# Feed-forward of a two-layer encoder: one 512-column product for both parts of an activation

## The chip, the cores and the metric

One core of a Trainium2 chip runs the whole program in one launch. The metric is the device time of that launch in microseconds (us). Kernels are compared by the median of several runs. The engines named here are TensorE (PE for its products, PEld for its weight loads), VectorE (DVE), ScalarE (ACT), GpSimd (POOL) and SyncE (SP), which issues nearly all DMAs.

## The reference

Two layers on 256 tokens of width 2048, in float32. Each layer is a token mixer (a gated MLP in layer 0, grouped-query attention in layer 1) followed by a feed-forward; a vector `c` gives each sub-layer a shift, a scale and a gate (`mod`).

```python
for i in range(DEPTH):                                   # DEPTH = 2
    mod = silu(c) @ w_ada[i] + b_ada[i]
    sh1, sc1, gt1, sh2, sc2, gt2 = split(mod, 6)
    h = rmsnorm(x, g_norm[i, 0]) * (1 + sc1) + sh1
    x = x + gt1 * (gmlp(h) if i == 0 else gqa(h))
    h = rmsnorm(x, g_norm[i, 1]) * (1 + sc2) + sh2
    a = h @ w_up[i]                                      # 2048 -> 2 * 5632
    a = cw[0] * a[t - 1] + cw[1] * a[t] + cw[2] * a[t + 1] + cb
    g, val = split(a, 2)
    x = x + gt2 * ((gelu(g) * val) @ w_down[i])          # 5632 -> 2048
return rmsnorm(x, g_final)
```

## The kernel before

**Layout and precision.** Channels lie on the 128 partitions and the 256 tokens (`S`) along the free dimension: `x` is 16 blocks (`NB`) of 128 x 256. Products run on operands of a rounded type (fp32r). To keep the accuracy each operand is split in two: `hi`, the rounded value, and `lo`, the rest. A product of a 128 x 128 weight block with an activation block is then three products that add up in PSUM (`prod_b`): weight hi with activation hi, weight hi with activation lo, weight lo with activation hi. Each has 256 columns and its own weight load. Below, a *block* is one such 128 x 128 weight block with all its products.

**Weights.** `weight` loads a raw tile of up to 2048 columns (5 such buffers), ACT casts it to `hi` in halves of 1024 columns and DVE subtracts to get `lo`; there are 5 half tiles of each. A half tile holds 8 blocks. SP issues the DMAs. The same raw buffers carry the rows of `w_ada`: `ada` reduces one such row block on DVE to 128 values of `mod` (192 of them). The list of all `ada` is worked off by `pump`, called by every `weight`: a credit grows by `state["rate"]` (the constants RO, RK, RU, RD, RW) and each whole credit issues one `ada`.

**Feed-forward** (`ffn`, once per layer). `new_h` and `make_h` give the activation, hi and lo in two tiles, each with rows padded by 8 elements here (`STEP`). The 5632 hidden channels are 44 blocks, each a pair (gate and value). The first 14 pairs begin in `outer`: tiles `pfa` (pairs 0 to 6, half of the sum) and `pfc` (pairs 7 to 13, all of it). Then seven calls of `up_rest` finish pairs 0 to 6, adding to a copy of `pfa` in SBUF (`part`, which is `yacc`), and `up_pair` makes the other 30 pairs (`pf`); both values of a pair share one PSUM bank of 512 columns. `epilogue` does the three-tap convolution, gelu and the product, and `split_f` the hi and lo of the result. The down projection (`pd`) runs in three parts of 16, 16 and 12 pairs (`PARTS`), each over 16 output blocks, once `LEAD` = 2 further pairs have been made; `residual` adds it to `x` (in layer 0 the first part waits in `yacc`). So the order of stages in a layer is pfa, pfc, up 0 (15 weight tiles), down 0 (16 tiles), up 1 (32), down 1 (16), up 2 (20), down 2 (16).

**Order.** The program is written as one sequence. A scheduler then orders the instructions of each engine by its own estimate of times; at run time every engine works strictly in that order. Work on a finished bank is put in `pend` and runs when the next `weight` has issued its casts.

Of the kernel before, what the change touches and what calls it, by code (L numbers as in the profile page):

```python
# [38 lines left out]
RK = ((0.75, 0.75, 0.75, 0.0), (0.6, 0.6, 0.6, 0.0))  # L39
RU = 0.75  # L40
RD = 0.85
RW = 0.5
# [9 lines left out]
def kernel(  # L52
# [20 lines left out]
    def bank(name, tag=None):  # L73
        return cur["ps"].tile([P, 512], F32, tag=tag or cur["tag"], name=name, bufs=cur["bufs"][tag or cur["tag"]])

    def phase(stack, name, nf, bufs={"ps": 8}, tag="ps", rt="ps"):

        cur["ps"] = stack.enter_context(tc.tile_pool(name=name + "_ps", bufs=1,
                                                     space=bass.MemoryType.PSUM, reuse_waits="tile"))
        cur["bufs"], cur["tag"], cur["rt"] = bufs, tag, rt  # L80
        cur["f"] = stack.enter_context(tc.tile_pool(name=name + "_f", bufs=nf, reuse_waits="tile"))
        cur["scr"] = stack.enter_context(tc.tile_pool(name=name, bufs=1, reuse_waits="tile"))
        return cur["scr"]
# [39 lines left out]
    cur["tag"], cur["bufs"] = "ps", {"ps": 2}  # L123
# [88 lines left out]


# [26 lines left out]
    def rstd_bcast(name, keep):  # L240

        pm = bank(f"pm_{name}", cur["rt"])
        r = tmp.tile([P, TC], F32, tag="r", name=f"r_{name}")
# [18 lines left out]
    def new_h(name, step=0):  # L262
        hts["hi"] = hbuf.tile([P, NB, S + step], F32R, tag="hhi", name=f"hhi_{name}")[:, :, :S]
        hts["lo"] = hbuf.tile([P, NB, S + step], F32R, tag="hlo", name=f"hlo_{name}")[:, :, :S]
        return hts["hi"], hts["lo"]
# [14 lines left out]
    def split_f(name, src):  # L280
        fbuf = cur["f"]
        fhi = fbuf.tile([P, S + STEP], F32R, tag="fhi", name=f"fhi_{name}")[:, :S]
        flo = fbuf.tile([P, S + STEP], F32R, tag="flo", name=f"flo_{name}")[:, :S]
        A.copy(fhi, src)
        V.tensor_tensor(out=flo, in0=src, in1=fhi.bitcast(F32), op=ALU.subtract)
        return fhi, flo
# [141 lines left out]
    def gqa(l, rstd):  # L428
        with ExitStack() as st:
# [17 lines left out]

            pk = [[bank(f"pk{t}_{n}", ("pb", "pa", "pb")[n]) for n in range(3)] for t in range(TC)]
# [35 lines left out]

            krot, rk = rope("k", [pk[t][0] for t in range(TC)], "k")
# [108 lines left out]
    def ffn(l, rstd, nxt, defer):  # L594
        with ExitStack() as st:
            ff = phase(st, f"ff{l}", FB)
            R = rstd()
            hhi, hlo = new_h(f"f{l}", STEP)
# [3 lines left out]
            def halves(b):  # L602
                return b[:, :S], b[:, S:]

# [45 lines left out]
            def up_rest(i):  # L650
                pb = bank(f"pf{l}_{i}")
                w = weight(wup2_d[l, i], 2 * (NB - H) * P)
                for s in range(2):
                    for k in range(NB - H):
                        prod_b(pb[:, s * S:(s + 1) * S], w((s * (NB - H) + k) * P, P), hhi[:, H + k, :],
                               hlo[:, H + k, :], k == 0 and s == 0, k == NB - H - 1)

                def fin():
                    V.tensor_tensor(out=part[:, i, :], in0=pb, in1=part[:, i, :], op=ALU.add)
                    fs[i] = epilogue(i, halves(part[:, i, :]))  # L660
# [3 lines left out]
            def up_pair(i):  # L664
                pb = bank(f"pf{l}_{i}")
                for s in range(2):
                    w = weight(wup1_d[l, i - 2 * KO, s], 2048)
                    for kb in range(NB):
                        prod_b(pb[:, s * S:(s + 1) * S], w(kb * P, P), hhi[:, kb, :], hlo[:, kb, :],
                               kb == 0 and s == 0, kb == NB - 1)  # L670

                def fin():
                    fs[i] = epilogue(i, halves(pb))

                pend.append(fin)
# [4 lines left out]
            for pi, nk in enumerate(PARTS):  # L680
# [11 lines left out]
                for j in range(NB):  # L692
# [3 lines left out]
                    for k in range(nk):  # L696
                        ks = k * P
                        prod_b(pd[:, :S], w(ks, P), fs[base + k][0], fs[base + k][1],
                               k == 0, k == nk - 1)

                    def fin(j=j, pd=pd, pi=pi):
                        if pi == 0 and defer:
                            A.copy(yacc[:, j, :], pd[:, :S])
                        else:
                            residual(l, GT2, j, pd[:, :S])
# [135 lines left out]
```

## Time and profile before

| | |
|---|---|
| median of 3 runs | 2147.91 us (2146.85 to 2148.34) |
| the profiled execution | 2148.5 us, of which the span is 2146.7 us |
| PE busy | 2081.6 us (97%), 16348 products |
| DVE busy | 1703.8 us (79%) |
| ACT busy | 1018.3 us (47%) |
| mean granted TensorE clock | 0.985 of full speed |
| HBM read | 575.99 MB |

Products are pipelined: a PE row lasts longer (282 ns on average for `pf`) than the time to the next one, so the pace of PE is read from the chain of waits, where a merged row gives a length and a number of products, and not from the mean duration. A stretch of the windows counts what falls into it, so its counts are a few more or less than a stage's.

### The profile page before, as it was taken

The page shows a single profiled execution, that of the slowest core. Times are in us where ns is not written, and L with a number is a line of the kernel's source. Part 1 is how long each engine was busy: PE and PEld are TensorE (multiplying, and loading weights), DVE is VectorE, ACT ScalarE, POOL GpSimd, SP SyncE. Part 2 cuts the span into 40 slices and gives each one's busy share as a digit, 9 for nine tenths or more (in the row PEclk, how much of TensorE's full clock was granted, in tenths as well). Part 3 has the DMA queues.
Part 4 walks back from the last instruction along what each step waited for, and adds up shares of the span by engine and source line. Part 5 has one row for each costly group of instructions (what it writes and reads, how often), then busy time and mean ns, then how long its engine had stood idle before and what let it go on. Part 6 is the DMA issues. An engine that isn't in the chain of part 4 may idle for free.

```text
span 2146.7 us, 39158 instructions
## 1 busy us (share of the span) xinstructions
PE 2081.6 (97%) x16348; PEld 2026.0 (94%) x16348; DVE 1703.8 (79%) x2258; ACT 1018.3 (47%) x1484; POOL 17.4 (1%) x15
## 2 busy tenths in 40 slices
PE   6899998999999999999999999899999999999997
PEld 6778998999999999999988789899999999999997
DVE  7998999899988999889986687866978666655665
ACT  3435433446544554345445654444653445434542
POOL 0000000000000000000000000000000000000000
PEclk8999999999999999999999999899999999999999
DMA  9998898985888889988966456678558655555542
GB/s 394 404 370 331 307 382 320 366 334 214 302 343 330 331 331 330 344 323 314 338 230 225 139 196 236 217 273 310 184 194 319 231 178 192 181 190 184 182 157 95
DMA packets 85137, 580.62 MB, mean 270 GB/s; under 512 B 9952, under 2 KB 11488, under 8 KB 25056
## 3 DMA queue, kind: packets, MB, share of 16 engines
q1 hardware_dynamic: 84528, 577.93, 72.8%
q8 instruction: 128, 2.10, 0.4%
q14 instruction: 49, 0.40, 0.0%
q10 hardware_dynamic: 432, 0.20, 0.0%
HBM read 575.99 MB, written 2.10 MB: 269 GB/s over the span
## 4 chain that ended last, share of the span: by engine, by line
PE 51%; issue 37%; DVE 7%; ACT 2%; DMA 2%; POOL 0%; SPq 0%; POOLq 0%; DVEq 0%; ACTq 0%
PE pf L205 18%; PE pd L205 12%; PE po L205 4%; DVE ada L140 3%; PE pw L205 3%; PE pk L205 3%; DVE lo L189 3%; PE pq L205 3%; PE pfc L205 3%; PE pfa L205 2%; PE pub L205 1%; ACT hi L188 1%; DMA w<-in_wu 1%; PE pqo L549 1%; DMA ada<-in_wada 1%
## 5 line engine op out<-in xcount | busy, mean ns | idle before, releaser
L188 ACT CAST hi<-w 128x1024 fp32r<-128x1024 f32 x740 | 739.5, 1009 | 892.0 <-PE pf L205 353.8
L189 DVE TENSOR_TENSOR lo<-w,hi 128x1024 fp32r<-128x1024 f32 x740 | 857.4, 1169 | 323.1 <-ACT hi L188 319.8
L205 PE MATMUL pf<-hhi_f,hi 128*128 128x256 f32 x2144 | 604.3, 282 | 0.0
L205 PE MATMUL pf<-hhi_f,lo 128*128 128x256 f32 x2144 | 601.1, 280 | 0.0
L205 PE MATMUL pf<-hlo_f,hi 128*128 128x256 f32 x2144 | 600.9, 280 | 0.0
L140 DVE CUSTOM_DVE_ANT_0 ada<-ada,cond_bc,bada 128x2048 f32<-128x2048 f32 x192 | 449.6, 2346 | 37.0 <-DMA ada<-in_wada 36.9
L205 PEld LDWEIGHTS pf<-hlo_f,hi 128*128 128x128 f32 x2144 | 404.8, 189 | 0.0
L205 PEld LDWEIGHTS pf<-hhi_f,lo 128*128 128x128 f32 x2144 | 404.3, 189 | 0.0
L205 PEld LDWEIGHTS pf<-hhi_f,hi 128*128 128x128 f32 x2144 | 403.8, 188 | 0.0
L205 PE MATMUL pd<-fhi_f,lo 128*128 128x256 f32 x1408 | 394.7, 282 | 0.0
L205 PE MATMUL pd<-flo_f,hi 128*128 128x256 f32 x1408 | 393.3, 280 | 0.0
L205 PE MATMUL pd<-fhi_f,hi 128*128 128x256 f32 x1408 | 391.5, 279 | 0.2 <-ACT hi L188 0.2
L205 PEld LDWEIGHTS pd<-fhi_f,hi 128*128 128x128 f32 x1408 | 264.9, 189 | 0.4 <-ACT hi L188 0.4
L205 PEld LDWEIGHTS pd<-fhi_f,lo 128*128 128x128 f32 x1408 | 264.6, 188 | 0.2
L205 PEld LDWEIGHTS pd<-flo_f,hi 128*128 128x128 f32 x1408 | 264.5, 188 | 0.0
L205 PE MATMUL pfc<-hlo_f,hi 128*128 128x256 f32 x448 | 123.4, 283 | 1.6 <-DVE hlo_f L277 1.6
L205 PE MATMUL pfc<-hhi_f,hi 128*128 128x256 f32 x448 | 123.3, 283 | 1.1 <-ACT hi L188 1.1
L205 PE MATMUL pfc<-hhi_f,lo 128*128 128x256 f32 x448 | 113.8, 282 | 0.0
L613 DVE SCALAR_TENSOR_TENSOR t<-pf,cw,t 128x255 f32<-128x255 f32 x240 | 102.2, 475 | 0.0
L205 PEld LDWEIGHTS pfc<-hlo_f,hi 128*128 128x128 f32 x448 | 85.3, 190 | 2.0 <-DVE hlo_f L277 2.0
L205 PEld LDWEIGHTS pfc<-hhi_f,hi 128*128 128x128 f32 x448 | 85.1, 190 | 1.3 <-ACT hi L188 1.3
L205 PEld LDWEIGHTS pfc<-hhi_f,lo 128*128 128x128 f32 x448 | 79.9, 190 | 0.2 <-DVE lo L189 0.2
(194 smaller groups left out, 2809.5 us busy)
## 6 DMA issues: line engine op xcount, KB each, us to landing
ada<-in_wada SPq DMA_DIRECT2D x192, 1024.0 KB, 6.5
w<-in_wup SPq DMA_DIRECT2D x134, 1024.0 KB, 4.9
w<-in_wdn SPq DMA_DIRECT2D x64, 1024.0 KB, 4.9
w<-in_wup SPq DMA_DIRECT2D x48, 896.0 KB, 6.2
w<-in_wdn SPq DMA_DIRECT2D x32, 768.0 KB, 4.3
w<-in_wu SPq DMA_DIRECT2D x16, 1024.0 KB, 7.9
w<-in_wv SPq DMA_DIRECT2D x16, 1024.0 KB, 7.2
w<-in_wout SPq DMA_DIRECT2D x16, 1024.0 KB, 6.8
```

The costliest lines, as they stand in the source:

```text
L140: V.tensor_tensor_reduce(out=w, in0=w, in1=cond_bc, op0=ALU.mult, op1=ALU.add, scale=1.0, scalar=bada[:, l, m:m + 1], accum_out=mod[:, l, ...
L188: A.copy(hi[:, :n], w[:, c:c + n])
L189: V.tensor_tensor(out=lo[:, :n], in0=w[:, c:c + n], in1=hi[:, :n].bitcast(F32), op=ALU.subtract)
L205: T.matmul(out, lhsT=a, rhs=b, start=start, stop=stop, skip_group_check=True)
L549: T.matmul(po, lhsT=va[:, kc, g * P:(g + 1) * P], rhs=ps_[h][:, kc, :], start=kc == 0, stop=kc == TC - 1)
L613: V.scalar_tensor_tensor(out=o[:, to], in0=a[:, frm], scalar=cw[:, l, tap, n:n + 1], in1=o[:, to], op0=ALU.mult, op1=ALU.add)
```

## The change

The hi and lo of an activation become the two halves of one tile (`hh` for `h`, `f` for the hidden channels), without the padding. `prod_w` takes the place of `prod_b` in `up_rest`, `up_pair` and the down projection: weight hi times the 512 columns of hi and lo at once, then weight lo times the 256 columns of hi. A block has two products and two weight loads instead of three, and the result is one bank whose two halves have still to be summed. `gather` does that with a copy on ACT and an add on DVE (into a new tile `ab`), `up_rest` with two adds instead of half of one, `residual` by being called twice. Each value of a pair has a bank of its own. `outer` and the mixers keep `prod_b`, but the feed-forward's `h` and the attention's output lose their padding too. The rates of `pump` change: in layer 0 lower in the feed-forward, then 0.3 in the first projection of the attention (`RP`), 0.75 instead of 0.5 in its last (`RW`), and in layer 1 higher in pfa and pfc (0.9) and 0.5 instead of 0 in up 0.

```diff
-RK = ((0.75, 0.75, 0.75, 0.0), (0.6, 0.6, 0.6, 0.0))
-RU = 0.75
-RD = 0.85
-RW = 0.5
+RK = ((0.75, 0.75, 0.75, 0.0), (0.9, 0.9, 0.9, 0.5))
+RU = 0.6
+RD = 0.65
+RP = 0.3
+RQ = 0.0
+RW = 0.75
...
+    def prod_w(out, w, xx, start, stop):
+
+        whi, wlo = w
+        mm(out, whi, xx, start, False)
+        mm(out[:, :S], wlo, xx[:, :S], False, stop)
...
-        hts["hi"] = hbuf.tile([P, NB, S + step], F32R, tag="hhi", name=f"hhi_{name}")[:, :, :S]
-        hts["lo"] = hbuf.tile([P, NB, S + step], F32R, tag="hlo", name=f"hlo_{name}")[:, :, :S]
+        hts["x"] = hbuf.tile([P, NB, 2 * S + step], F32R, tag="hh", name=f"hh_{name}")
+        hts["hi"], hts["lo"] = hts["x"][:, :, :S], hts["x"][:, :, S:2 * S]
...
-        fhi = fbuf.tile([P, S + STEP], F32R, tag="fhi", name=f"fhi_{name}")[:, :S]
-        flo = fbuf.tile([P, S + STEP], F32R, tag="flo", name=f"flo_{name}")[:, :S]
+        f = cur["f"].tile([P, 2 * S], F32R, tag="f", name=f"f_{name}")
+        fhi, flo = f[:, :S], f[:, S:2 * S]
...
+            state["rate"] = RP
...
+            def gather(out, b):
+
+                A.copy(out, b[:, S:])
+                add(out, b[:, :S])
+
+            def add(t, b):
+                V.tensor_tensor(out=t, in0=b, in1=t, op=ALU.add)
...
             def up_rest(i):
-                pb = bank(f"pf{l}_{i}")
+                pb = [bank(f"pf{l}_{i}_{s}") for s in range(2)]
                 w = weight(wup2_d[l, i], 2 * (NB - H) * P)
                 for s in range(2):
                     for k in range(NB - H):
-                        prod_b(pb[:, s * S:(s + 1) * S], w((s * (NB - H) + k) * P, P), hhi[:, H + k, :],
-                               hlo[:, H + k, :], k == 0 and s == 0, k == NB - H - 1)
+                        prod_w(pb[s], w((s * (NB - H) + k) * P, P), hx[:, H + k, :], k == 0, k == NB - H - 1)
 
                 def fin():
-                    V.tensor_tensor(out=part[:, i, :], in0=pb, in1=part[:, i, :], op=ALU.add)
-                    fs[i] = epilogue(i, halves(part[:, i, :]))
+                    src = halves(part[:, i, :])
+                    for s in range(2):
+                        add(src[s], pb[s][:, S:])
+                        add(src[s], pb[s][:, :S])
+                    fs[i] = epilogue(i, src)
...
             def up_pair(i):
-                pb = bank(f"pf{l}_{i}")
+                ab = []
                 for s in range(2):
+                    pb = bank(f"pf{l}_{i}_{s}")
                     w = weight(wup1_d[l, i - 2 * KO, s], 2048)
                     for kb in range(NB):
-                        prod_b(pb[:, s * S:(s + 1) * S], w(kb * P, P), hhi[:, kb, :], hlo[:, kb, :],
-                               kb == 0 and s == 0, kb == NB - 1)
...
+                        prod_w(pb, w(kb * P, P), hx[:, kb, :], kb == 0, kb == NB - 1)
+
+                    def fin(s=s, pb=pb):
+                        if s == 0:
+                            ab.append(ff.tile([P, 2 * S], F32, tag="ab", name=f"ab{l}_{i}", bufs=1))
+                        gather(halves(ab[0])[s], pb)
+                        if s == 1:
+                            fs[i] = epilogue(i, halves(ab[0]))
...
-                        prod_b(pd[:, :S], w(ks, P), fs[base + k][0], fs[base + k][1],
-                               k == 0, k == nk - 1)
+                        prod_w(pd, w(ks, P), fs[base + k][2], k == 0, k == nk - 1)
...
                         if pi == 0 and defer:
-                            A.copy(yacc[:, j, :], pd[:, :S])
+                            gather(yacc[:, j, :], pd)
                         else:
+                            residual(l, GT2, j, pd[:, S:])
                             residual(l, GT2, j, pd[:, :S])
```

Two places show how the order moves. The first is PE at the start of down 0 in layer 1. In the rows, `pd1_0_0` is the bank of layer 1, part 0, output block 0, `f1_0` the hidden block of pair 0, and `hi271_0` the first half of weight tile 271, the first tile of that stage. Before:

```order
L205 MATMUL pd1_0_0_17207<-fhi_f1_0_16246,hi271_0_17186 128x256
L205 MATMUL pd1_0_0_17207<-flo_f1_0_16247,hi271_0_17186 128x256
L205 MATMUL pd1_0_0_17207<-fhi_f1_0_16246,lo271_0_17187 128x256
L205 MATMUL pd1_0_0_17207<-fhi_f1_1_16319,hi271_0_17186 128x256
L205 MATMUL pd1_0_0_17207<-flo_f1_1_16320,hi271_0_17186 128x256
L205 MATMUL pd1_0_0_17207<-fhi_f1_1_16319,lo271_0_17187 128x256
```

Now:

```order
L207 MATMUL pd1_0_0_15435<-f_f1_0_14641,hi271_0_15413 128x512
L207 MATMUL pd1_0_0_15435<-f_f1_0_14641,lo271_0_15414 128x256
L207 MATMUL pd1_0_1_15483<-f_f1_0_14641,hi272_0_15473 128x512
L207 MATMUL pd1_0_1_15483<-f_f1_0_14641,lo272_0_15474 128x256
L207 MATMUL pd1_0_0_15435<-f_f1_1_14704,hi271_0_15413 128x512
L207 MATMUL pd1_0_0_15435<-f_f1_1_14704,lo271_0_15414 128x256
L207 MATMUL pd1_0_1_15483<-f_f1_1_14704,hi272_0_15473 128x512
L207 MATMUL pd1_0_1_15483<-f_f1_1_14704,lo272_0_15474 128x256
```

Each weight block has two rows instead of three, and where before all 16 pairs of output block 0 came first, two output blocks now take turns, pair by pair, up to pair 5; pair 6 and the others follow.

The second is DVE at the end of up 0 in layer 1, from the last half tile of weight 270, the last tile of that stage; `t1_15` is the convolution of pair 15, `ada1_94` a row block of `w_ada`. Before:

```order
L189 TENSOR_TENSOR lo270_1024_17133<-w270_17126,hi270_1024_17132 128x1024
L616 TENSOR_TENSOR t1_15_16935<-t1_15_16935 128x256
L189 TENSOR_TENSOR lo271_0_17187<-w271_17184,hi271_0_17186 128x1024
L613 SCALAR_TENSOR_TENSOR t1_16_17065<-pf1_16_16924,cw_92,t1_16_17065 128x255 x2
L285 TENSOR_TENSOR flo_f1_15_16945<-t1_15_16935,fhi_f1_15_16944 128x256
L613 SCALAR_TENSOR_TENSOR t1_16_17065<-pf1_16_16924,cw_92,t1_16_17065 128x255 x2
L189 TENSOR_TENSOR lo271_1024_17191<-w271_17184,hi271_1024_17190 128x1024
L616 TENSOR_TENSOR t1_16_17065<-t1_16_17065 128x256
L189 TENSOR_TENSOR lo272_0_17259<-w272_17256,hi272_0_17258 128x1024
L285 TENSOR_TENSOR flo_f1_16_17075<-t1_16_17065,fhi_f1_16_17074 128x256
L189 TENSOR_TENSOR lo272_1024_17263<-w272_17256,hi272_1024_17262 128x1024
L189 TENSOR_TENSOR lo273_0_17319<-w273_17316,hi273_0_17318 128x1024
```

Now:

```order
L191 TENSOR_TENSOR lo270_1024_15373<-w270_15366,hi270_1024_15372 128x1024
L292 TENSOR_TENSOR f_f1_0_14641<-t1_0_14632,f_f1_0_14641 128x256
L631 SCALAR_TENSOR_TENSOR t1_1_14695<-yacc_13080,cw_92,t1_1_14695 128x255 x2
L191 TENSOR_TENSOR lo271_0_15414<-w271_15411,hi271_0_15413 128x1024
L631 SCALAR_TENSOR_TENSOR t1_1_14695<-yacc_13080,cw_92,t1_1_14695 128x255
L631 SCALAR_TENSOR_TENSOR t1_2_14755<-yacc_13080,cw_92,t1_2_14755 128x255
L631 SCALAR_TENSOR_TENSOR t1_1_14695<-yacc_13080,cw_92,t1_1_14695 128x255
L631 SCALAR_TENSOR_TENSOR t1_2_14755<-yacc_13080,cw_92,t1_2_14755 128x255
L142 ISA ada1_94_15561,mod_94<-ada1_94_15561,cond_bc_101,bada_82 128x2048
L142 ISA mod_94 128x1
L191 TENSOR_TENSOR lo271_1024_15418<-w271_15411,hi271_1024_15417 128x1024
L631 SCALAR_TENSOR_TENSOR t1_2_14755<-yacc_13080,cw_92,t1_2_14755 128x255
```

Before, the epilogues here are those of the last two pairs of the part and of the `LEAD`. Now they are those of pairs 0 to 6: `f_f1_0` to `f_f1_6` come behind this half tile, and an `ada` stands between them.

## Rows read from the trace of the kernel before

**Rows 1.** Part 1 of the page: busy time, share of the span, instructions of each engine.

```profile
PE 2081.6 (97%) x16348; PEld 2026.0 (94%) x16348; DVE 1703.8 (79%) x2258; ACT 1018.3 (47%) x1484; POOL 17.4 (1%) x15
```

**Rows 2.** Chain that ended last, in time: start us, us, what, instructions merged.

```profile
31.95 2.36 DVE lo L189 x2
...
453.35 2.26 DVE ada L140
...
458.35 6.64 PE pfc L205 x41
...
550.16 90.49 PE pd L205 x768
640.65 181.76 PE pf L205 x1536
822.41 90.56 PE pd L205 x768
```

**Rows 3.** Busy time by stretch: length; PE, PEld, DVE, ACT, POOL; PEclk, DMA, GB/s.

```profile
380.00:464.90 84.90, 82.23 (x675) 81.47 (x674) 76.52 (x89) 37.15 (x49) 0.00 (x0) 0.98 0.96 365
464.90:550.10 85.20, 85.20 (x722) 85.20 (x721) 79.62 (x128) 53.33 (x86) 0.00 (x0) 1.00 0.67 241
550.10:640.60 90.50, 90.50 (x770) 90.50 (x769) 79.13 (x94) 42.78 (x62) 0.00 (x0) 1.00 0.87 328
640.60:822.40 181.80, 181.80 (x1539) 181.80 (x1538) 166.92 (x219) 91.02 (x126) 0.00 (x0) 1.00 0.88 329
...
1026.50:1095.00 68.50, 68.31 (x577) 67.87 (x576) 64.80 (x88) 32.61 (x45) 0.00 (x0) 1.00 0.92 345
1366.00:1382.00 16.00, 8.14 (x57) 7.68 (x55) 11.76 (x19) 4.30 (x8) 0.70 (x1) 0.74 0.65 226
...
1504.00:1589.00 85.00, 85.00 (x721) 85.00 (x720) 75.94 (x134) 56.82 (x95) 0.00 (x0) 1.00 0.53 186
...
1679.40:1861.20 181.80, 181.80 (x1539) 181.80 (x1538) 112.44 (x155) 90.33 (x124) 0.00 (x0) 1.00 0.53 186
```

**Rows 4.** Groups by line and form: the counts of the feed-forward products.

```profile
L205 PE MATMUL pf<-hhi_f,hi 128*128 128x256 f32 x2144 | 604.3, 282 | 0.0
...
L205 PE MATMUL pd<-fhi_f,hi 128*128 128x256 f32 x1408 | 391.5, 279 | 0.2 <-ACT hi L188 0.2
```

**Rows 5.** The same chain, in the mixer stages: products of 512 and 256 columns.

```profile
220.55 16.32 PE pub L205 x136
...
1100.80 67.11 PE pk L205 x288
1167.91 12.70 PE pq L205 x56
...
1302.47 45.49 PE pw L205 x387
```

**Rows 6.** Groups by line and form: VectorE and ScalarE work around the feed-forward.

```profile
L189 DVE TENSOR_TENSOR lo<-w,hi 128x1024 fp32r<-128x1024 f32 x644 | 782.5, 1221 | 283.4 <-ACT hi L188 280.2
...
L140 DVE CUSTOM_DVE_ANT_0 ada<-ada,cond_bc,bada 128x2048 f32<-128x2048 f32 x192 | 449.6, 2346 | 37.0 <-DMA ada<-in_wada 36.9
...
L291 DVE SCALAR_TENSOR_TENSOR x<-pd,mod,x 128x256 f32<-128x256 f32 x80 | 38.3, 482 | 24.1 <-PE pd L205 22.5
...
L285 DVE TENSOR_TENSOR flo_f<-t,fhi_f 128x256 fp32r<-128x256 f32 x88 | 36.7, 417 | 0.9 <-ACT fhi_f L284 0.9
...
L703 ACT COPY yacc<-pd 128x256 f32<-128x256 f32 x16 | 5.9, 367 | 0.0
```

**Rows 7.** VectorE in order of time, around the first down projection of layer 0.

```profile
537.94 0.88 DVE L613 SCALAR_TENSOR_TENSOR t<-yacc,cw,t 128x255 f32<-128x255 f32 x2
...
539.07 1.22 DVE L189 TENSOR_TENSOR lo<-w,hi 128x1024 fp32r<-128x1024 f32 x1
...
565.67 0.42 DVE L285 TENSOR_TENSOR flo_f<-t,fhi_f 128x256 fp32r<-128x256 f32 x1
```

## What the change does to the time: the prediction

> **What bounds the kernel now.** I read the page's first part, then the chain that ended last, then the busy time by stretch, then the groups by form. In the first part the reader is to see PE at 97% and DVE at 79% [rows 1]. The chain says the same stage by stage: in the feed-forward it consists of long unbroken PE pieces (pd, pf, pd) that join without a gap [rows 2]. An exception lies ahead of them: near 453 us, in pfc of layer 0, the chain runs over an `ada` on DVE before it comes back to PE [rows 2]; that stretch takes 84.9 us with PE busy for 82.2 [rows 3]. The stretches then show how much room DVE has under PE: in layer 0 little (79.6 of 85.2 us in up 0, 166.9 of 181.8 in up 1, 64.8 of 68.5 in down 2), in layer 1 much (112.4 of 181.8 in up 1), except in up 0, where it is busy for 75.9 of 85.0 [rows 3]. So PE's pace sets the time, and DVE is a close second at the beginning of each feed-forward.
>
> **PE's pace, before and after.** A block of `pf` takes three products: 3 x 181.76/1536 = 0.3550 us; one of `pd` 3 x 90.56/768 = 0.3538 us [rows 2]. The new block is a product of 512 columns and one of 256. The feed-forward has no product of 512, but the attention has, with a weight load for each: `pq` took 12.70/56 = 0.2268 us and `pk`, waits included, 67.11/288 = 0.2330 [rows 5]. The tiles now lie unpadded. Of 256 columns on unpadded tiles the trace has `pub`, 16.32/136 = 0.1200, against 0.1183 for the padded `pf` [rows 2, 5]. I take 0.2268 + 0.1200 = 0.3468 us, since `pq` runs unbroken and both its operands are unpadded too. The ends: with pk's value 0.3530; and if the lack of padding costs nothing, 1.7 ns less for each product, 0.3434.
>
> There are 2144 blocks of `pf` and 1408 of `pd` (one hi-hi product for each [rows 4]). They give back 2144 x 0.0082 = 17.6 and 1408 x 0.0070 = 9.8, together 27.4 us. Against that stand the products that stay at 256 columns and lose their padding: the 1008 of pfa and pfc in layer 1 and the 336 of pfa in layer 0 at 1.7 ns (pfc there partly waits for DVE), and the 768 of `pw`, which go from 45.49/387 = 0.1175 to 0.1200 [rows 5]: 1.7 + 0.6 + 1.9 = 4.2 us. PE alone would be 23.2 us faster.
>
> By the Trainium skill ("TensorE: Matmul & The Clock Gate", Back-to-back issue gap) a warm product occupies its columns at 2.4 GHz plus about 2.5 ns; that speaks against the change, since a block would give back only those 2.5 ns, 8.9 us over 3552 blocks, an estimate by that page. The rows disagree with the page: 256 columns more cost 0.2268 - 0.1183 = 0.1085 us, so that 0.0098 us of a product of 256 does not grow with its columns.
>
> **What is added elsewhere.** Each value of a pair needs a copy on ACT (0.367 us for this size) and an add on DVE of 256 columns (0.417, from the like-sized subtraction of `split_f`), and most outputs of the down projection a second `residual` (0.482) [rows 6]. ACT hides its part: in up 1, 32 copies of 0.37 make 12 us more on 91 of 181.8 [rows 3]. On DVE 32 adds make 13.3 us in up 1 of layer 0, but by the order only 19 `ada` stand there instead of 24, at 2.35 us each [rows 6] 11.7 less. This holds for the rest of layer 0 too: up 0 to down 2 have 63 `ada` where there were 79. In down 2, where DVE gets about 4 us more and the room was 3.7, half tiles made ahead cover what is missing; if they did not, it would cost 2 us. In up 1 to down 2 of layer 1 there is room for everything.
>
> The `ada` go elsewhere: pk gets 4 (0 before), pw 12 (9), pfa and pfc of layer 1 20 (12), up 0 of layer 1 8 (0), down 0 there 2 (9). In pfa and pfc the stretch carries 24 weight tiles of 0.9 MB and 20 MB of `ada` in about 122 us, some 350 GB/s, which pfc of layer 0 surpassed at 365 [rows 3]: hidden by PE. Around the start of that feed-forward PE already stands for half of the time (8.14 of 16.0 us busy [rows 3]), and DVE has one `ada` more in the neighbourhood: I charge 1 us (ends 0 and 2.3).
>
> **The new wait.** It comes at the start of down 0, and the order rows in the section on the change show it. DVE makes the half tiles and finishes the epilogues in one fixed order. In layer 0 now, the last half tile of up 0 was ready at 539.07 + 1.22 = 540.29 [rows 7] and down 0 began at 550.16 [rows 2]: DVE leads by 9.9 us. Its limit is 5 half tiles of 8 blocks, 13.9 us at the new pace.
>
> In layer 1 the new order puts between the last half tile of up 0 and the result of pair 3 (`f_f1_3`): 5 half tiles at 1.18 (2.36 for two [rows 2]), 2 `ada` at 2.26 [rows 2], 16 convolution steps at 0.44 (0.88 for two [rows 7]) and 8 operations of 256 columns at 0.42 [rows 6]: 5.9 + 4.5 + 7.0 + 3.4 = 20.8 us. To pair 5 it is another 8 steps and 4 operations, 5.2 us: 26.0. As a test, the same count in layer 0 now, from that half tile to pair 15 (8 half tiles, 3 `ada`, 13 steps, 7 operations) gives 24.9, and the trace has 565.67 + 0.42 - 540.29 = 25.8 [rows 7]. PE wants pair 3 after 6 blocks of down 0, at 9.9 + 2.1 = 12.0: it waits 8.8 us. It then wants pair 5 four blocks later, at 22.2, and waits 3.8. Together 12.6 us (with a lead of 13.9 us 8.6; with half the lead 17.6). Behind the waiting product stands all of PE; nobody makes the loss good, since PE sets the time afterwards.
>
> In layer 0 the new order has 5 half tiles, 2 `ada`, 12 steps and 6 operations ahead of pair 6: 18.2 us. PE wants it after 12 blocks, at 9.9 + 4.2 = 14.1, and waits 4.1 (ends 0.1 and 9).
>
> **The sum**, against the profiled execution of 2148.5 us (span 2146.7 and 1.8 around it; the median of the runs shown is 0.6 lower): 2148.5 - 23.2 + 12.6 + 4.1 + 1.0 = 2143.0 us.
>
> **Rivals.** (1) The waits do not show: DVE's lead is larger than I think because its operations overlap, or the pairs are ready in time. For it: before, nothing waits at this place, though pair 15 came nearly 16 us after down 0 of layer 0 began. Against it: pair 15 was wanted late there, pair 3 is wanted at once. Time 2148.5 - 23.2 + 1 = 2126. (2) The padding has no part in it, for instance because a product of 512 columns starts half as often on a tile. Blocks of 0.3434 give 2144 x 0.0116 + 1408 x 0.0104 = 39.5 us and the 4.2 us fall away: 2148.5 - 39.5 + 17.7 = 2127. Against it: `pub` and `pq` agree on about 13 ns a product beyond the columns, at 0.1067 us for 256 of them at full clock. (3) Slower: DVE becomes the bound from pfa to down 0 in both layers. For it: pfc of layer 0, with 25 `ada` in its 24 tiles, lost 5.4 us (84.9 against 672 x 0.1183), and layer 1 now gets 20. Its up 0 needs 75.9 + 8 x 2.34 for the `ada` + 7.8 for the adds - 19.2 for epilogues put off = 83.2 us of DVE under 240 x 0.3468 = 83.2 of PE, so a lead once lost is not regained; up 0 of layer 0 likewise. With half the lead both waits grow by 5, pfc of layer 1 loses 5.4 and down 2 of layer 0 its 2: 2143.0 + 10 + 5.4 + 2 = 2160. It decides once DVE's work in up 0 exceeds PE's. (4) The long product costs what `pk` showed: 2144 x 0.0020 + 1408 x 0.0008 = 5.4 us back, and 2148.5 - 5.4 + 4.2 + 17.7 = 2165. Against it: pk's row holds its waits for `make_h`. By the Trainium skill's gap, cited above, the time would be 2148.5 - 8.9 + 4.2 + 17.7 = 2162.
>
> **How the numbers follow.** My forecast 0.45 (its own range 2136 to 2151), rival 1 0.15, rival 2 0.13, rival 3 0.17, rival 4 0.10. What a measurement can tell is 0.2%, 4.3 us: faster means below 2143.6, slower above 2152.2. The forecast lies at that edge; I split it into 0.24 faster, 0.19 same and 0.02 slower. Rivals 1 and 2 are faster, 3 and 4 slower but for 0.05: faster 0.52, same 0.24, slower 0.24. The range 2118 to 2161 leaves out rival 4 and the outer edges of rivals 1 to 3.
>
> **What would show it.** In the chain after, a `pf` stage should run at 0.347 us a block (177.6 us for up 1). Then PE should stand for about 12 us at the start of down 0 in layer 1, released by DVE's last subtraction of a pair, and for about 4 us in layer 0. Blocks of 0.343 would refute the price of the padding, an unbroken chain at that place the wait, gaps in pfc or up 0 of layer 1 would point to rival 3. If DVE's `ada` released PE anywhere in up 1, my account of the room there would be wrong.

## The result, and the profile after

The changed kernel takes 2175.0 us (median of 4 runs, 2169.4 to 2180.4), the kernel before 2147.6 in the same runs: ratio 1.0122, 95% interval 1.0109 to 1.0136. It is 1.2% slower; the forecast was 2143.0 us, the range 2118 to 2161. The profiled execution took 2176.1 us, its span 2174.2: 27.5 us more than before. The runs of the new kernel also lie 11 us apart, those of the old one 1.5.

Part 1 of its page, beside [rows 1]: PE has the same busy time in fewer instructions, DVE 96 us more.

```profile
PE 2083.1 (96%) x12796; PEld 1862.5 (86%) x12796; DVE 1800.0 (83%) x2516; ACT 1060.7 (49%) x1604; POOL 19.4 (1%) x15
```

The chain of the same stages as in [rows 2] (start us, us, what, instructions): up 1 of layer 0 runs at 2 x 177.49/1024 = 0.3467 us a block, the forecast value (0.3468), and down 1 at 2 x 88.75/512 = 0.3467.

```profile
643.26 177.49 PE pf L207 x1024
820.75 88.75 PE pd L207 x512
```

The busy time by stretch, with the columns of [rows 3], shows what came of it elsewhere. In order: up 0, down 0, up 1 and down 2 of layer 0; up 0, down 0 and up 1 of layer 1.

```profile
466.10:551.20 85.10, 84.96 (x482) 73.48 (x481) 80.92 (x142) 53.22 (x84) 0.00 (x0) 1.00 0.64 229
551.30:643.10 91.80, 89.84 (x514) 77.69 (x513) 81.94 (x116) 46.41 (x71) 0.00 (x0) 1.00 0.80 292
643.10:820.60 177.50, 177.50 (x1027) 155.23 (x1026) 166.26 (x238) 102.55 (x156) 0.00 (x0) 1.00 0.83 307
1020.30:1090.80 70.50, 67.85 (x386) 58.50 (x384) 65.31 (x93) 31.91 (x43) 0.00 (x0) 1.00 0.86 307
1517.70:1604.50 86.80, 84.87 (x482) 73.43 (x481) 85.09 (x135) 46.43 (x68) 0.00 (x0) 1.00 0.77 284
1604.50:1707.50 103.00, 93.86 (x514) 80.53 (x513) 75.80 (x120) 49.33 (x71) 0.00 (x0) 0.95 0.52 180
1707.50:1888.40 180.90, 180.90 (x1026) 156.87 (x1025) 127.86 (x188) 100.48 (x156) 0.00 (x0) 1.00 0.53 186
```

Up 1 has the same 512 blocks in both layers, the same full clock and PE busy throughout, yet 177.5 us in layer 0 and 180.9 in layer 1, and there DVE is idle for nearly a third of the time. So the block itself has two paces. Start to start of the first products of blocks, in PE's order of time (start us, us, what), first in layer 0, then in layer 1:

```profile
699.95 0.39 PE L207 MATMUL pf<-hh_f,hi 128*128 128x512 f32 x1
...
700.30 0.40 PE L207 MATMUL pf<-hh_f,hi 128*128 128x512 f32 x1
...
700.65 0.39 PE L207 MATMUL pf<-hh_f,hi 128*128 128x512 f32 x1
...
1799.73 0.40 PE L207 MATMUL pf<-hh_f,hi 128*128 128x512 f32 x1
...
1800.10 0.40 PE L207 MATMUL pf<-hh_f,hi 128*128 128x512 f32 x1
...
1800.44 0.40 PE L207 MATMUL pf<-hh_f,hi 128*128 128x512 f32 x1
...
1800.80 0.40 PE L207 MATMUL pf<-hh_f,hi 128*128 128x512 f32 x1
```

In layer 0 a block takes 0.35 us each time; in layer 1 it takes 0.37, 0.34, 0.36 in turn. I call the first the fast rhythm (0.3467 us) and the second the slow one (2 x 180.9/1024 = 0.3533). The slow one gives back almost nothing against 0.3550 before [rows 2]. A stage keeps its rhythm for hundreds of blocks; in this execution it changes near a stall of PE or at the border of a stage. Up 0 of layer 0 and nearly all of layer 1's feed-forward run in the slow one.

Where the 27.5 us are, stage by stage (after minus before, from the starts of the stages):

| stretch | before | after | difference |
|---|---|---|---|
| to up 0 of layer 0 | 464.8 | 466.1 | +1.3 |
| up 0, down 0 of layer 0 | 175.7 | 177.0 | +1.3 |
| up 1, down 1, up 2 of layer 0 | 385.9 | 377.2 | -8.7 |
| down 2 to the first of `pk` | 74.4 | 83.8 | +9.4 |
| `pk` to `pfa` of layer 1 | 281.1 | 291.3 | +10.2 |
| pfa, pfc, up 0 of layer 1 | 207.1 | 209.2 | +2.1 |
| down 0 of layer 1 | 90.5 | 103.0 | +12.5 |
| up 1, down 1, up 2 of layer 1 | 385.9 | 384.4 | -1.5 |
| down 2 to the end | 81.4 | 82.2 | +0.8 |

The loss at down 0 of layer 1 begins with the wait that the prediction named. The waits of PE there (us in total, times, longest) are released by DVE's subtraction of a pair:

```profile
PE pd L207 <- DVE f_f L292: 9.1, 3, 5.7
```

They come before pairs 2, 3 and 5 and last 1.2, 5.7 and 2.3 us. The stage takes 14.2 us more than the 88.75 of an undisturbed down 1 in layer 0, so 5 us are something else. The granted clock is 0.95 in the mean of this stage, where every other feed-forward stage shown has 1.00. In stretches of 4 us it is at half, 1.2 instead of 2.4 GHz, just behind the longest standstill, and again behind the last one:

```profile
1608.00:1612.00 4.00, 0.27 (x2) 0.00 (x0) 4.00 (x8) 0.79 (x2) 0.00 (x0) 0.74 0.42 113
1612.00:1616.00 4.00, 2.06 (x6) 1.77 (x7) 3.65 (x10) 3.12 (x7) 0.00 (x0) 0.50 0.56 227
...
1620.00:1624.00 4.00, 4.00 (x16) 3.42 (x16) 3.38 (x8) 2.99 (x8) 0.00 (x0) 0.57 0.00 0
```

About nine blocks ran at half clock, at 0.64 us each some 3 us more than at full clock; the slow rhythm in the rest of the stage is 1.4 (both worked out from the starts of the products).

What was not foreseen stands ahead of `pk`. The chain after runs there over the loads of the rope tables; DVE multiplies three of them ahead of the first `ht_b`, and each load is issued only behind the multiply before it:

```profile
1093.64 0.34 DVE tbqc L452
...
1094.00 5.18 DMA gbqs<-in_gq
...
1099.72 2.82 DMA gbkc<-in_gk
...
1102.98 0.49 DVE ht_b L282
```

In the kernel before DVE multiplies one table ahead of `ht_b`, and the chain has no table at that place; it runs over the statistics of the norm:

```profile
1098.46 1.24 PE pr_mx L126 x4
...
1099.72 0.49 DVE ht_b L274
```

Between `pk` and `pfa` 4.6 of the 10.2 us are lost in the heads of the attention, from the end of `pk` to the closed run of `pw`, first before, then after:

```profile
1168.00:1302.10 134.10, 130.09 (x708) 111.71 (x707) 99.98 (x194) 82.95 (x219) 9.17 (x5) 0.99 0.48 172
```

```profile
1171.50:1310.20 138.70, 130.31 (x684) 111.56 (x683) 101.88 (x195) 81.95 (x218) 11.15 (x5) 0.96 0.47 174
```

PE's waits there double, from 4.0 to 8.4 us, and what releases it are steps of the attention on ACT and DVE, no `ada`. Another 4.4 us are in the closed run of `pw`: about 1.6 of them the missing padding, the rest some 23 more products, which did not fit into the heads. About 1 us is at the border to `pfa`.

### The profile page after: what moved, and what is told of

The parts are those of the page before. It is cut to its first block, busy times and chain, and to the rows that moved or that the text cites. A ratio compares the mean times of both kernels' runs of the same rounds, so it can differ in the third digit from the quotient of the medians.

```text
span 2174.2 us, 32412 instructions
## 1 busy us (share of the span) xinstructions
PE 2083.1 (96%) x12796; PEld 1862.5 (86%) x12796; DVE 1800.0 (83%) x2516; ACT 1060.7 (49%) x1604; POOL 19.4 (1%) x15
## 4 chain that ended last, share of the span: by engine, by line
PE 47%; issue 38%; DVE 9%; DMA 4%; ACT 2%; POOL 0%; DVEq 0%; SPq 0%; POOLq 0%; ACTq 0%
PE pf L207 16%; PE pd L207 10%; PE po L207 4%; DVE ada L142 4%; DVE lo L191 4%; PE pk L207 3%; PE pq L207 3%; DMA ada<-in_wada 3%; PE pfc L207 3%; PE pw L207 2%; PE pfa L207 2%; PE pub L207 2%; ACT hi L190 1%; PE pqo L558 1%; DMA w<-in_wu 0%
## 5 line engine op out<-in xcount | busy, mean ns | idle before, releaser
L207 PE MATMUL pf<-hh_f,hi 128*128 128x512 f32 x2144 | 752.2, 397 | 2.1 <-ACT hi L190 1.0
L207 PE MATMUL pf<-hh_f,lo 128*128 128x256 f32 x2144 | 598.9, 279 | 0.0
L207 PE MATMUL pd<-f_f,hi 128*128 128x512 f32 x1408 | 496.7, 398 | 10.6 <-DVE f_f L292 10.5
L207 PEld LDWEIGHTS pf<-hh_f,hi 128*128 128x128 f32 x2144 | 402.5, 188 | 100.1 <-issue 1.8
L207 PEld LDWEIGHTS pf<-hh_f,lo 128*128 128x128 f32 x2144 | 404.1, 188 | 0.0
L207 PE MATMUL pd<-f_f,lo 128*128 128x256 f32 x1408 | 393.4, 281 | 3.2 <-DVE lo L191 3.2
L207 PEld LDWEIGHTS pd<-f_f,hi 128*128 128x128 f32 x1408 | 265.1, 189 | 75.6 <-DVE f_f L292 12.4
L207 PEld LDWEIGHTS pd<-f_f,lo 128*128 128x128 f32 x1408 | 266.6, 189 | 5.1 <-DVE lo L191 4.2
L207 PE MATMUL pfc<-hh_f,hi 128*128 128x256 f32 x896 | 157.7, 285 | 2.5 <-DVE hh_f L285 1.4
L207 PEld LDWEIGHTS pfc<-hh_f,hi 128*128 128x128 f32 x896 | 135.8, 194 | 3.1 <-DVE hh_f L285 1.8
```

The costliest lines, as they stand in the source:

```text
L207: T.matmul(out, lhsT=a, rhs=b, start=start, stop=stop, skip_group_check=True)
```

## Experiments

The theory at first: (i) the new rates of the `ada` cost what layer 0 gains (the end of layer 0, `pk` to `pfa`, the wait in layer 1); (ii) the slow rhythm eats the gain of layer 1. The rival: the new products with their adds and banks cost it, wherever the `ada` stand. Ratios are to the kernel before, measured on the same chip, with 95% intervals; a kernel without one was run once. The diffs are shortened, with lines joined by `;`.

**The changed kernel with the old rates (a_oldrates).**

```diff
-RK = (..., (0.9, 0.9, 0.9, 0.5)); RU = 0.6; RD = 0.65; RP = 0.3; RW = 0.75
+RK = (..., (0.6, 0.6, 0.6, 0.0)); RU = 0.75; RD = 0.85; RP = 0.0; RW = 0.5
```

> The changed kernel with the old rates of the ada stream (no rate of its own for the pk and rope stages). Theory 1 (the new rates cost the end of layer 0 and the stretch from pk to layer 1's feed-forward, some 18 us of the 27 lost): those stretches come back to the times of before, and the wait at down 0 of layer 1 falls from 12.6 us to below 6; up 1 of layer 0, where DVE gets 13.3 us of adds more on 166.9, becomes DVE-bound at about 180 instead of 177.5. Time 2145 to 2155. Rival (the products and the adds cost it wherever the ada stand): 2168 to 2178.

2164.3 us, ratio 1.0068 (1.0051 to 1.0085): between the two. Layer 1 is good (up 1 177.4, no wait at down 0: 89.0 us), but layer 0 loses 20 us, in two places that I had not expected: down 0 and down 2. Stretches, then PE's waits at the two places:

```profile
549.50:648.60 99.10, 92.08 (x515) 79.89 (x514) 90.64 (x124) 46.86 (x72) 0.00 (x0) 0.95 0.82 306
...
1029.70:1111.60 81.90, 72.92 (x386) 61.41 (x385) 76.10 (x118) 35.81 (x53) 0.00 (x0) 0.94 0.79 283
```

```profile
PE pd L207 <- DVE f_f L292: 7.0, 2, 5.4
...
PE pd L207 <- DVE lo L191: 5.7, 3, 2.8
```

**The kernel before with the new rates (b_newrates)**: the edit reversed, with the lines that set RP and RQ.

```diff
-RK = (..., (0.6, 0.6, 0.6, 0.0)); RU = 0.75; RD = 0.85; RW = 0.5
+RK = (..., (0.9, 0.9, 0.9, 0.5)); RU = 0.6; RD = 0.65; RP = 0.3; RQ = 0.0; RW = 0.75
```

> The kernel before with the new rates, and its old products. Theory 1: the rates alone cost 15 to 20 us at the end of layer 0 and from pk to layer 1's feed-forward, whatever the products: 2162 to 2168, no wait at down 0 of layer 1 above 5 us, since no adds stand in DVE's order. Rival (the adds and the new products make the loss): 2146 to 2151.

2176.2 us, ratio 1.0124 (1.0109 to 1.0139). The rates alone cost as much as the whole change, more than I expected. The gap ahead of `pk` (last product of down 2 to the first of `pk`) is 13.5 us, as in the changed kernel (13.3; 5.8 before), but for another reason: DVE multiplies one table there, as before, and waits for the load of an `ada`, which the rate RP puts ahead of the norm's statistics:

```profile
1094.61 7.71 DMA ada<-in_wada
...
1104.81 0.34 DVE tbqc L447
```

`pk` to `pfa` takes 289.0 us, and down 0 of layer 1 waits without a single second-half add (the expectation had less than 5 us there). The stage loses 9 us though PE stands for only 2.8 of them; the granted clock then falls to half, and 16 products take the 4 us in which 36 went before:

```profile
1604.10:1703.50 99.40, 96.60 (x771) 94.69 (x770) 66.42 (x98) 46.03 (x63) 0.00 (x0) 0.95 0.50 181
```

```profile
1600.00:1604.00 4.00, 4.00 (x36) 4.00 (x36) 3.50 (x6) 2.35 (x4) 0.00 (x0) 1.00 1.00 414
...
1608.00:1612.00 4.00, 1.85 (x10) 1.36 (x9) 4.00 (x8) 1.65 (x5) 0.00 (x0) 0.77 0.30 76
1612.00:1616.00 4.00, 4.00 (x16) 3.52 (x17) 3.79 (x11) 2.86 (x7) 0.00 (x0) 0.50 0.44 186
1616.00:1620.00 4.00, 4.00 (x16) 3.47 (x16) 3.42 (x9) 2.65 (x7) 0.00 (x0) 0.50 0.00 0
```

**The kernel before, unpadded (b_unpad).**

```diff
-        fhi = fbuf.tile([P, S + STEP], ...); flo = fbuf.tile([P, S + STEP], ...)
+        fhi = fbuf.tile([P, S], ...); flo = fbuf.tile([P, S], ...)
-            hhi, hlo = new_h(f"f{l}", STEP)
+            hhi, hlo = new_h(f"f{l}")
```

> The kernel before, with the h tile and the halves of an activation in the feed-forward unpadded, nothing else. If the padding is worth the 1.7 ns a product that the rows of pf and pub differ by, all 10656 products of the feed-forward lose it, 18 us: 2164 to 2168. Rival (the padding plays no part, and pub is slower for another reason): 2146 to 2150.

2159.3 us, ratio 1.0050 (1.0033 to 1.0067): between the two. The chain shows why: `pf` lost its 1.7 ns (184.32/1536 = 0.1200 us), `pd` nothing (90.45/768 = 0.1178).

```profile
641.51 184.32 PE pf L205 x1536
825.83 90.45 PE pd L205 x768
...
1308.22 30.39 PE pw L205 x268
```

`pw` even became faster, 30.39/268 = 0.1134 against 0.1175 [rows 5]. So it is not the padding as such. What differs is where the rows lie: in the built program all weights of this kernel are at 192 bytes modulo 256, h at 192 as well, the unpadded activations of `pd` and `pw` at 0. In the kernel before, padding spreads the rows over all multiples of 32 bytes, and single products of `pf` come at 114 to 124 ns: the distance between a product's activations and the next product's weights, modulo 2048 bytes, accounts for 94% of the variance of these times (worked out from the starts of 6414 products and the program's addresses). That alone does not show the cause: the distances name nearly each place in the loop (48 values for 72 places), and the place accounts for as much. The runs with moved addresses below test it.

**The changed kernel, padded (a_pad).**

```diff
-        f = cur["f"].tile([P, 2 * S], F32R, ...)
+        f = cur["f"].tile([P, 2 * S + STEP], F32R, ...)
-            hhi, hlo = new_h(f"f{l}")
+            hhi, hlo = new_h(f"f{l}", STEP)
```

> The changed kernel with 8 columns of padding behind each pair of halves (h tile and activation tile). If padding prices a product: the 2112 products of 256 columns in pfa, pfc and pw go back from 0.120 to 0.118 us, 4 us, and the two-product block may lose 1.7 to 3.4 ns (6 to 12 us): 2159 to 2171 by the two. If the slow rhythm of the block in layer 1 (0.3534 us instead of 0.3468) comes from where the rows lie, it goes away too, 9 us more. Rival (padding plays no part): 2170 to 2180.

2173.8 us, ratio 1.0118 (1.0103 to 1.0133), no difference in time. But the two rhythms are gone: with the rows spread, up 1 runs at 2 x 179.61/1024 = 0.3508 us a block, and layer 1 the same (179.5).

```profile
642.39 179.61 PE pf L207 x1024
```

**Old rates in layer 1 alone (a_rk1).**

```diff
-RK = ((0.75, 0.75, 0.75, 0.0), (0.9, 0.9, 0.9, 0.5))
+RK = ((0.75, 0.75, 0.75, 0.0), (0.6, 0.6, 0.6, 0.0))
```

> The changed kernel with the old rates of the ada in layer 1's feed-forward (0.6, 0.6, 0.6, 0.0 for 0.9, 0.9, 0.9, 0.5), all else as changed. Theory 1 (the wait at down 0 of layer 1 comes from the 8 ada that the new rate puts into up 0 of layer 1): down 0 goes from 103.0 back to about 89 to 91 us, and the whole to 2160 to 2164. Rival A (the adds of the second halves make the wait, since they stand in the same order on DVE): down 0 stays above 98 us and the time at 2172 to 2177. In the kernel before with the new rates down 0 took 99 us without any adds, which speaks for theory 1.

2156.6 us, ratio 1.0031 (1.0019 to 1.0042): 18 us better than the change. Down 0 of layer 1 has no wait left, with all its adds:

```profile
1606.50:1697.40 90.90, 90.81 (x515) 78.51 (x514) 89.80 (x119) 41.36 (x53) 0.00 (x0) 1.00 0.88 336
```

So the wait needs the new rates in layer 1; the adds alone don't make it. Which of these rates matters is seen from two runs below: up 0 has 8 `ada` on DVE in the changed kernel and 3 here; a_mid and b_rurd have 3 there too but 19 in pfa and pfc, one more than the changed kernel, and PE waits 1.2 us at down 0 in a_mid and not at all in b_rurd. That leaves the `ada` in up 0. In this execution layer 1 then ran in the fast rhythm (up 1 177.4), which is the rest of the 18 us.

**Three products in layer 0, two in layer 1, old rates (mix1).**

```diff
+            wide = l == 1      # else up_rest, up_pair and down as in the kernel before
-            hhi, hlo = new_h(f"f{l}")
+            step = cur["step"] = 0 if wide else STEP
+            hhi, hlo = new_h(f"f{l}", step)
```

> Old rates; the three products and the padding of before in layer 0, the two products, unpadded, in layer 1. Theory 1 (the two products pay where DVE has room, and layer 0 has none): layer 0 ends as before (last product of down 2 to first of pk 5.8 us, pk at about 1101), layer 1 from up 0 to down 2 takes 619 us as with the old rates in both layers instead of 629.4. Time 2138 to 2142; if layer 1 falls into the slow rhythm (0.3534 us a block), 2146 to 2150. Rival (the old rates with the new products cost 15.7 us for another reason than DVE in layer 0): 2150 to 2160.

2139.9 us, ratio 0.9955 (0.9938 to 0.9972), as expected; its four runs lie 1.8 us apart. Layer 1 is in the fast rhythm from the beginning of down 0 into down 2:

```profile
1679.30:1856.80 177.50, 177.50 (x1027) 155.22 (x1026) 127.83 (x188) 100.42 (x156) 0.00 (x0) 1.00 0.55 190
```

**Old rates, without the second halves' adds (a_noadd).**

```diff
-                A.copy(out, b[:, S:])
-                add(out, b[:, :S])
+                A.copy(out, b[:, :S])
-                        add(src[s], pb[s][:, S:])
-                            residual(l, GT2, j, pd[:, S:])
```

> The changed kernel with the old rates, without the second halves' adds and copies: the right half of each product (the hi part of the weights on the low part of the activation) is left unread, so its terms are missing from the output; all products and banks stay. Theory 1 (in layer 0 it is DVE's second-half adds that hold PE up): down 0 of layer 0 takes about 89 us instead of 99.1, down 2 about 70 instead of 81.8, and pk starts near 1095 instead of 1121; the whole takes 2136 to 2144. Rival (the two banks that a pair now takes, or the wider products themselves): layer 0 stays within 5 us of 1121.

2137.1 us. Layer 0 is whole again: down 0 and down 2 take 89.3 and 67.6 us instead of 99.1 and 81.9, and `pk` starts at 1090.4. With all banks and wide products in place, the 20 us that a_oldrates lost there are DVE's adds, with the order that they make. (Layer 1 ran in the slow rhythm here, 180.9 us for up 1, so the whole time understates the gain.)

```profile
548.60:637.90 89.30, 89.30 (x515) 78.36 (x514) 79.56 (x95) 44.29 (x67) 0.00 (x0) 1.00 0.87 327
...
1015.10:1082.70 67.60, 67.07 (x386) 58.46 (x385) 63.68 (x85) 31.60 (x43) 0.00 (x0) 1.00 0.95 349
```

**Only RU and RD as changed (a_mid).**

```diff
-RP = 0.3; RW = 0.75
+RP = 0.0; RW = 0.5      # and RK of layer 1 as in a_rk1
```

> The changed kernel with the old rates in layer 1 and also in the stages between (RP 0.0 for 0.3, RW 0.5 for 0.75); only RU and RD, in layer 0, stay as changed. Theory 1 (RP makes the tables for rope late, 7 to 8 us ahead of pk, and RW costs the output projection and its border 2 to 4): 2145 to 2150, with the last product of down 2 to the first of pk 6 us instead of 13. Rival (the ada that layer 0 no longer takes have to go somewhere, and cost the same in pk, rope or layer 1 wherever they go): 2154 to 2160.

2164.0 us, ratio 1.0068 (1.0051 to 1.0085): my theory on RP and RW fell. The gap ahead of `pk` is still 11.5 us, over the same two loads, and `pk` to `pfa` takes 291.8.

```profile
1101.66 3.56 DMA gbqs<-in_gq
...
1105.76 2.81 DMA gbkc<-in_gk
```

That it is slower than a_rk1 is the rhythm: this execution was in the slow one in both layers.

**RU and RD alone in the kernel before (b_rurd).**

```diff
-RU = 0.75; RD = 0.85
+RU = 0.6; RD = 0.65
```

> The kernel before with RU 0.6 and RD 0.65 alone (layer 0 takes fewer ada), all other rates and the three products as before. Theory 1c (the ada that layer 0 does not take cost about as much from pk to layer 1's feed-forward wherever they are put there): pk to pfa of layer 1 takes 287 to 292 us instead of 281.1, the whole 2156 to 2164. Rival (RP and RW, or the second-half adds, are needed for the loss): 2147 to 2152.

2157.3 us, ratio 1.0040 (1.0026 to 1.0055): within the expectation, at its low end. `pk` to `pfa` takes 285.8 us against 281.1, less than the 287 to 292 expected, and the gap ahead of `pk` grows by only 1.6. The first row is this kernel, the second the kernel before:

```profile
1101.80:1387.60 285.80, 270.12 (x1593) 239.80 (x1593) 209.34 (x344) 147.73 (x314) 9.86 (x6) 0.97 0.56 199
```

```profile
1100.80:1381.90 281.10, 269.25 (x1592) 238.70 (x1592) 206.33 (x341) 147.68 (x314) 9.87 (x6) 0.97 0.56 199
```

In the kernel before, taking `ada` out of layer 0 thus costs 9 of the 27.5 us by itself, and RK, RP and RW the other 19.

**Addresses moved (a_resid, a_resid2 from the old-rates version; b_resid from b_unpad).** The h tile of each layer starts OH floats later, and a filler of OF floats lies ahead of down's activation tiles.

```diff
+    OH, OF = (16, 48), (32, 8)      # a_resid2: (40, 56), (48, 24); b_resid: (16, 32), (16, 32)
-        hts["x"] = hbuf.tile([P, NB, 2 * S + step], ...)
+        raw = hbuf.tile([P, NB * 2 * S + 64], ...)
+        hts["x"] = raw[:, o:o + NB * 2 * S].rearrange("p (j c) -> p j c", c=2 * S)
```

> The changed kernel with the old rates, and the activations' addresses moved against the weights': the h tile of the feed-forward by 64 bytes in layer 0 and 192 in layer 1, the activation tiles of down by 128 and 32 bytes; weights stay at multiples of 256. Theory 1b (what a product costs beyond its columns, and the rhythm of the block, come from where the moving rows lie against the weights that are loaded meanwhile): the four kinds of stage show block times that differ from each other and from 0.3467 and 0.3534 us, each steady, somewhere in 0.333 to 0.360. Rival (the rhythm is a matter of chance after a wait, addresses play no part): every stage is at 0.3467 or 0.3534.

> The changed kernel with the old rates and four more addresses of the activations against the weights' (modulo 256): the h tile at 160 bytes in layer 0 and 224 in layer 1, down's tiles at 192 in layer 0 and 96 in layer 1. If the address sets the rhythm of the two products, each stage of a layer keeps one pace in all its parts outside of stalls, and one of the four may lie below 0.3467 us (0.333 to 0.345); if chance, stages at the same address differ, at 0.3467 or 0.3534.

> The kernel before, unpadded, with the activations' addresses moved against the weights': h lies 64 bytes off in layer 0 and 128 in layer 1, the activation tiles of down 128 and 192 (modulo 256; they were at 0 and 64, with 120.0 and 117.8 ns a product). Theory 1b: pf leaves its 120.0 ns in both layers, towards the 113.3 ns of pw at 64; the four values differ. Rival (addresses play no part): pf stays at 120.0, pd at 117.8.

2163.4, 2159.9 and 2143.1 us. A stage's block of two products, by the distance to the weights (modulo 256): 64: 0.353 us; 96: 0.350; 128: 0.351; 160: 0.3467; 192: 0.3534; 224: 0.3467 (but 0.353 in up 0); 32: 0.3467. In a_resid, layer 1 went from one to the other at every border, in all its parts, up at 192 and down at 32 bytes:

```profile
1698.10:1879.00 180.90, 180.90 (x1026) 157.12 (x1025) 127.88 (x188) 100.53 (x156) 0.00 (x0) 1.00 0.52 186
1879.00:1967.80 88.80, 88.80 (x515) 78.71 (x514) 55.32 (x68) 35.12 (x36) 0.00 (x0) 1.00 0.53 190
```

Three products at 64 bytes take 0.3533 us a block (180.91/1536 x 3), at 128 0.356, at 192 0.3533 and, in down 2 of layer 1, 0.340. So addresses take part, against the rival; none made two products cheaper than 0.3467; and that one address shows two paces (two products at 224 here, and at 0 in layers 0 and 1 of the changed kernel; three products at 192) is against my own theory that each is steady.

**Addresses chosen, three products in layer 0 and two in layer 1 (best), and three in both (best3).**

```diff
-            step = cur["step"] = 0 if wide else STEP
-            hhi, hlo = new_h(f"f{l}", step)
+    OH, OF = (48, 8), (48, 8)       # and a filler of 16 floats ahead of the heads' tiles
# best3:
-    OH, OF = (48, 8), (48, 8)
+    OH, OF = (48, 48), (48, 48)
-            wide = l == 1
+            wide = False
```

> As the mixed version (three products in layer 0, two in layer 1, old rates), unpadded, with the addresses chosen by residues modulo 256 against the weights': layer 0's activations at 192 bytes, layer 1's at 32, the heads' at 64. If addresses set the pace: pfa and pfc of layer 1 leave 120.0 ns, pw goes to 113 to 114 ns (2.6 us), layer 0's products to 117.8 or less (2 us and more), layer 1 stays in the fast rhythm in all six stages: 2130 to 2138. Rival (chance): 2138 to 2150.

> The last version with three products in layer 1 as well, all activations of the feed-forward at 192 bytes modulo 256 against the weights' 0; the products are those of the kernel before. If the address sets the pace of three products: layer 1 runs at 0.3400 us a block as layer 0 did, 6.7 ns under the two products, 1776 blocks, 12 us: 2094 to 2100. Rival (layer 0's pace had to do with its order, and layer 1's three products stay at 117.8 ns, 0.3534 us): 2118 to 2124.

best took 2109.9 us (2106.4 to 2127.1), ratio 0.9836 (0.9795 to 0.9877), far below the range expected: layer 0's three products fell to 174.08/1536 = 0.1133 us, 0.3400 a block, under the two products' 0.3467 in layer 1.

```profile
629.09 174.08 PE pf L209 x1536
```

best3 took 2105.8 us (2093.1 to 2122.3), ratio 0.9789 (0.9721 to 0.9857). Layer 1 did as the address theory says; but layer 0, at the same address, was slow this time. Up 1 of both layers, 512 blocks at full clock:

```profile
638.90:819.70 180.80, 180.80 (x1538) 180.80 (x1537) 166.72 (x217) 90.94 (x125) 0.00 (x0) 1.00 0.88 330
1666.40:1840.50 174.10, 174.10 (x1539) 174.10 (x1538) 111.45 (x155) 90.44 (x124) 0.00 (x0) 1.00 0.55 195
```

The pace also changes within one execution. In down 2 of layer 0, at one address and full clock, best goes from 113.3 to 117.8 ns a product behind some stalls of PE, and best3 from 117.8 to 113.3 (worked out from the starts of the products). Whether best or best3 is faster can't be told (the intervals overlap). So one of the two fastest versions has the products of the kernel before, and no part of the change but the joined, unpadded tile.

## Why the prediction was wrong

**The price of the block** (0.3468 us, 27.4 us back) was right in size where it held: 0.3467 in up 1, down 1 and up 2 of layer 0. It failed as a fixed price. In nearly all of layer 1 the same block took 0.3533, and up 1, down 1 and up 2 gained 1.5 us there, where layer 0 gained 8.7 on the same blocks. I had taken `pq` and `pub` as samples of one cost per product; the runs show a cost that depends on the addresses and on a rhythm that a stall can change. Rival 4 had 0.3530 for the block, near the slow rhythm, for another reason. The Trainium skill ("TensorE: Matmul & The Clock Gate", Back-to-back issue gap) has a formula for a single product that would give about 109 ns for 256 columns, an estimate; no stage here came below 113.3.

**The padding** (4.2 us) came out as priced in pfc of layer 1 and the unbroken part of `pw`, 0.1200 us both, but for a reason that is not the padding: `pd` without it kept 0.1178.

**The wait at down 0 of layer 1** (12.6 us) came at the place, before the pairs and with the releaser named, but smaller: 5.7 us before pair 3 for 8.8 forecast, 2.3 before pair 5 for 3.8, and 1.2 before pair 2, together 9.1. By the prediction's terms the stage would have taken 88.8 + 12.6 = 101.4 us; that it took 103.0 is partly luck, since some 3 us are the clock, which I had left out, and 1.4 the slow rhythm. Nor did I say which part of DVE's order decides: it is the `ada` of up 0. With all 8 of them the stage loses 9 us with the old products and without any add; with 3 of them the adds cost next to nothing.

**Layer 0's wait** (4.1 us) came at its place too, before pair 6, but PE waited only 1.4 us there for the pair; with shorter pauses later, among them 0.5 us for a half tile behind an `ada` load, the stage took 3.1 over an undisturbed down. The sum is near, its parts are not.

**The step that failed most is "hidden by PE".** For the `ada` moved out of layer 0 the sum had 1.0 us. The end of layer 0 up to `pk` lost 9.4 us and `pk` to `pfa` 10.2, of which the unpadded `pw` is 1.9: 17.7 us. I priced these `ada` by DVE's busy time and the transfer rate of pfa and pfc, and never looked at what stands in one order with them between the layers, where PE already waits. How more `ada` lengthen the waits in the heads, where none of them releases PE, stays open. b_newrates loses 7.0 and 7.9 us in these two stretches without any new product, and b_rurd shows that taking the `ada` out of layer 0 costs 9 us even with all other rates as before. The two kernels don't lose the gap ahead of `pk` in the same way, though: with the old products it is an `ada` load, in the changed kernel the rope tables. The cover in down 2 ("half tiles made ahead") was also wrong: the stage took 70.5 us, not 67. Rival 3 named DVE as the bound from pfa on, and DVE was busy for 85.1 of 86.8 us in up 0 of layer 1; it had neither the stretch between the layers nor the rhythm.

From the forecast's -5.5 to the measured +27.5 are 33 us, by stretch (measured less the forecast's terms there): layer 1's feed-forward 13.3, of which the slow rhythm is some 11; the end of layer 0 10.7 (9.4 and the pace's gain that did not come); `pk` to `pfa` 7.3; layer 0 up to the end of down 0 1.7.

What the runs leave open: what decides which rhythm a stage falls into after a stall (best and best3 differ in it at one address), and what makes the scheduler put rope tables ahead of `ht_b`. It puts three there in the changed kernel, a_pad, a_rk1 and a_mid, two in a_oldrates, a_resid and a_resid2, and one, as before, in a_noadd and in every version with the old products in layer 0; so the adds in layer 0 take part, and RU and RD with them.

## What to carry to other kernels

Work that is moved off a busy stage is not free where it lands: price the landing place by what stands in one queue with it, and try the schedule and the arithmetic apart, since here each alone made the kernel slower (27.5 and 15.7 us) for different reasons, and both together cost 27.5, not the sum. Before products are joined to save their overhead, look whether one stage's products take the same time in every stage of the profile: where equal work shows two paces, the overhead is not a constant, and moving a tile by some bytes may be worth more than the new arithmetic (2106 to 2110 us against 2140).

## What the runs showed of the hardware

Streams of products with full clock and PE always busy ran at a few steady paces: 256 columns at 113.3, 117.8, 118.7 and 120.0 ns a product, blocks of 512 and 256 mostly at 346.7 or 353.3, and at 350 to 351 at two addresses and with padding. The distance between activations and weights in their memory, modulo 256 bytes, takes part in it (for three products at 0 only 120.0 was seen, at 192 113.3 or 117.8), but does not settle it alone. A stage keeps its pace, and changes were seen behind stalls and at borders of stages. The runs of the changed kernel, a_rk1, best and best3 lie 11 to 29 us apart, those of the kernel before and of mix1 2 to 5; that the rhythm makes this spread is likely but not shown, since one execution of each was profiled. Standstills of 2.8 us in the stage of 99.4 us were followed by some 10 us at half the granted clock, and the stage lost 6 us beyond the standstills, twice as much as they lasted.
